# RWKV-7's 32 x 32 blocks: through DRAM and two chains, or through TensorE and one

## The chip, the cores and the metric

The kernel runs on one core of a Trainium2 chip. The metric is the device time of one execution in microseconds (us). Engines: TensorE (PE; its weight loads are PEld), VectorE (DVE), ScalarE (ACT), GpSimd (POOL) and SyncE (SP), each with its own queue of instructions in order. The program is written against a framework that fixes, before the run, in which order each engine gets its instructions: what is written first has priority, and what is written later is moved into the gaps that the framework expects.

## The reference

The input x is [1, 512, 1024]: 512 tokens of 1024 features. A first block has three branches behind one projection (a state space branch, RWKV-7 and HGRN-2), gates, an output projection and a feed-forward part; two layers of a second block with four other branches follow. The change lies in RWKV-7 alone: 8 heads of 64 features, forward and backward over the tokens.

```
def step(s, inp):
    r_t, w_t, k_t, v_t, kk_t, a_t = inp
    sa = jnp.einsum('bhvk,bhk->bhv', s, -kk_t)
    s = (s * w_t[:, :, None, :] + sa[..., None] * (kk_t * a_t)[:, :, None, :]
         + v_t[..., None] * k_t[:, :, None, :])
    return s, jnp.einsum('bhvk,bhk->bhv', s, r_t)
```

In chunks of 64 tokens this becomes products of matrices, with one inverse per chunk, head and direction: (I + A)^-1, where A is strictly triangular, 64 x 64.

## The kernel before

The stage under study runs from about 30 to 690 us of 3645. `rwkv` handles four tiles j of two heads. For each: `rwkv_in` (projections, normalised keys), `rwkv_decays`, `rwkv_mid` (all causal products of the 8 chunks and the inverses), `rwkv_scan` (8 chunks one after the other, both directions side by side) and `rwkv_out`. The inputs of tile j + 1 are written inside the scan of tile j. Behind all of RWKV, in lower priority, stand four heads of `hgrn` and 16 tiles of `gates` with tiles and PSUM banks of their own (bg, H): they fill gaps. The next stage (`ssd`) takes over the memory of this one.

In `rwkv_mid`, G[128, 32, 128] holds for each of 32 matrices m (direction, chunk, head) the products of sources i (partitions) by targets t (L424, L427). The two 32 x 32 diagonal blocks q of each 64 x 64 part have to be inverted. Forward substitution wants one block per partition, with all its elements in a row:

- L432: two DMAs write the blocks of G into the DRAM array pd; L441: two DMAs read them into M, block (q, m) on a partition, and again on the other 64 partitions.
- X0 and X1 (L436 to L443) begin as the unit matrix. Rows 4 a + 2 c + q of the inverse: c names one of two independent chains, q the half of the partitions.
- L458 to L466: for each of 31 columns i, both chains multiply (L463, into tx0, tx1) and both subtract (L466): 120 instructions of VectorE, products of column i of X with row i of M, inner runs of neighbours.
- L470: four DMAs write X to pd2; L473: two DMAs read it back into G, element (r, m, t) to partition r.
- L475 to L491: the block above the diagonal, -X1 A12 X2, for 16 matrices at a time: 16 transposes (L480) and a copy (L482) give X1 transposed, then 16 products (L485), a scaled copy (L487), 16 products (L490), a copy into G (L491).

Memory of a bank (512 float32 columns in PSUM) comes by use: S has two banks, T, O and H one, acc one.

Of the kernel before, what the change touches and what calls it, by code (L numbers as in the profile page):

```python
# [32 lines left out]
def blocks(*ws):  # L33
    """[K, N] matrices with N a multiple of 128 -> units of 8 blocks of 128 x 128, each
    unit with its rows on the partitions; the blocks run over columns, then rows."""
    seq = []
    for w in ws:
        k, n = w.shape
        seq.append(w.reshape(k // 128, 128, n // 128, 128).transpose(2, 0, 1, 3).reshape(-1, 128, 128))
    b = np.concatenate(seq) if len(seq) > 1 else seq[0]  # L40
    return np.ascontiguousarray(b.reshape(-1, UB, 128, 128).transpose(0, 2, 1, 3))


def paired(a, b):
    """Blocks of two matrices, a column tile of each in turn."""
    k, n = a.shape
    s = np.stack([w.reshape(k // 128, 128, n // 128, 128).transpose(2, 0, 1, 3) for w in (a, b)], axis=1)
    s = s.reshape(-1, UB, 128, 128)
    return np.ascontiguousarray(s.transpose(0, 2, 1, 3))


def parts(n):
    """(from, how many) of n pairs of row tiles, up to four at a time."""
# [4 lines left out]
def sevens(w0, w1):  # L58
    """Pairs of column tiles, one of each matrix [K, N]: for up to four pairs of row tiles
    (even, odd) at a time, the first tile's even and the second's even blocks, then the second's  # L60
    odd and the first's odd blocks, with the rows on the partitions."""
# [9 lines left out]
def gate_up(a, name, *ws):  # L71
    """The column tiles FF7 for products in sevens, the others for plain ones."""
# [5 lines left out]
def odd_even(w):  # L78
    """The odd and the even column tiles."""
# [5 lines left out]
#: Column tiles of the second block's w_in (without the 16 mLSTM gates) in the order of use.  # L85
# [9 lines left out]
#: The same for the first block's (without the 32 steps of the state space branch).  # L95
# [8 lines left out]
def first_constants():  # L104
    """Selectors of heads and masks of the chunks' orders."""
# [16 lines left out]
class Packed:  # L122
    """Small vectors side by side in one array; the program finds them by name."""
# [33 lines left out]
def nat_masks():  # L157
    """0 inside the window of 16 columns, -1e30 outside: 128 queries (16 columns by 8 rows) by
    256 keys (32 columns by 8 rows), for the first, the middle and the last query tiles."""
# [10 lines left out]
def arrange(x):  # L170
    """The kernel's inputs as the program reads them."""
# [55 lines left out]
def run(gen):  # L227
    """A generator's work at once; its result."""
# [6 lines left out]
class First:  # L235
    """The first block's layer: state space (SSD), RWKV-7 and HGRN-2 branches."""
# [4 lines left out]
    def conv_pad(self, ps, side):  # L241
        """psum / rms with zeros on either side."""
# [8 lines left out]
    def shifted(self, it, n, out):  # L251
        """Token shift in both directions of column tile n."""
# [6 lines left out]
    def half_sigmoid(self, out, ps, hb):  # L259
        """0.5 + 0.5 tanh: the sigmoid of (psum / WS + bias), hb half the bias."""  # L260
# [14 lines left out]
    def rwkv(self, yd):  # L275
        """Chunks of 64 tokens, both directions side by side, a tile of two heads after the
        other; the backward direction keeps its keys and values reversed within the chunks."""
# [46 lines left out]
    def rwkv_in(self, j, it, lx):  # L324
        """What a tile of two heads needs of the projections."""
# [37 lines left out]
    def rwkv_decays(self, j, lx):  # L363
        """exp of the decays' running sums (and of their negatives) as seen from the middle of
        a chunk, |exponent| < 19.5; the state's scale from one chunk's middle to the next's."""
# [30 lines left out]
    def rwkv_mid(self, j):  # L396
        """Keys and queries with their decays, all causal products of a chunk, (I + A)^-1."""
# [17 lines left out]
        # (source: b or k, i) x (target: kk or r, t) for every direction, chunk and head  # L415
# [12 lines left out]
        # the 32 x 32 diagonal blocks of I + A inverted, one block's even or odd rows a partition  # L428
        pd = self.t(self.dram, [2, 32, 32, 32], "pd")
        for q in range(2):  # L430
            s = slice(32 * q, 32 * q + 32)
            nc.scalar.dma_start(out=pd[q].rearrange("m i t -> i m t"), in_=G[s, :, s])  # L432
        M = self.t(mid, [128, 1024], "M").rearrange("p (i t) -> p i t", i=32)
        tx = [self.t(mid, [128, 80], f"tx{c}") for c in range(2)]
        # rows 4 a + 2 c + q: two independent chains c, each on the halves q of the partitions
        X = [self.t(mid, [128, 8, 32], f"X{c}") for c in range(2)]  # L436
        for c in range(2):
            nc.gpsimd.memset(X[c], 0.0)
        for q in range(2):
            s = slice(64 * q, 64 * q + 64)  # L440
            (nc.scalar, nc.sync)[q].dma_start(out=M[s], in_=pd.rearrange("q m i t -> (q m) i t"))  # L441
            for c in range(2):
                nc.gpsimd.memset(X[c].rearrange("p a b -> p (a b)")[s, 2 * c + q::36], 1.0)  # L443
        # values by token on the upper partitions
# [13 lines left out]
        for i in range(31):  # L458
            ts, nt = slice(i + 1, 32), 31 - i
            rs = [(c, (i - 2 * c) // 4 + 1) for c in range(2) if i >= 2 * c]  # L460
            for c, n in rs:
                t = tx[c][:, 0:n * nt].rearrange("p (a b) -> p a b", b=nt)
                v.tensor_tensor(out=t, in0=X[c][:, 0:n, i:i + 1].to_broadcast([128, n, nt]), in1=M[:, i:i + 1, ts].to_broadcast([128, n, nt]), op=ALU.mult)  # L463
            for c, n in rs:
                t = tx[c][:, 0:n * nt].rearrange("p (a b) -> p a b", b=nt)
                v.tensor_tensor(out=X[c][:, 0:n, ts], in0=X[c][:, 0:n, ts], in1=t, op=ALU.subtract)  # L466
        pd2 = self.t(self.dram, [2, 32, 8, 2, 2, 32], "pd2")
        for q in range(2):
            for c in range(2):
                nc.scalar.dma_start(out=pd2[:, :, :, c, q].rearrange("q m r t -> (q m) r t"), in_=X[c][64 * q:64 * q + 64])  # L470
        for q in range(2):
            s = slice(32 * q, 32 * q + 32)
            nc.scalar.dma_start(out=G[s, :, s], in_=pd2[q].rearrange("m r c e t -> (r c e) m t"))  # L473
        # the block above the diagonal: -X1 A12 X2
        lo, hi = slice(0, 32), slice(32, 64)  # L475
        for q in range(2):
            ms = range(16 * q, 16 * q + 16)
            px = self.b("S")
            for n, m in enumerate(ms):
                nc.tensor.transpose(px[lo, 32 * n:32 * n + 32], G[lo, m, lo], self.ident[lo, lo])  # L480
            st = self.w()
            nc.scalar.copy(out=st[lo], in_=px[lo])  # L482
            px = self.b("S")
            for n, m in enumerate(ms):
                mm(px[hi, 32 * n:32 * n + 32], lhsT=G[lo, m, hi], rhs=st[lo, 32 * n:32 * n + 32], start=True, stop=True)  # L485
# [8 lines left out]
    def rwkv_scan(self, j):  # L494
# [10 lines left out]
        for c in range(NC):  # L505
# [9 lines left out]
            # B v + K z = -(I + A) u on the lower, B' v + R z on the upper partitions  # L515
# [13 lines left out]
            if not last:  # L529
                # the next state, one head's values beside the other's, zero across heads  # L530
# [1617 lines left out]
```

## Time and profile before

| | |
|---|---|
| median of 3 runs | 3642.4 us (3641.06 to 3648.86) |
| profiled execution: span from first to last instruction | 3644.9 us |
| TensorE busy | 3388.2 us, 93% |
| VectorE busy | 2751.5 us, 75% |
| ScalarE busy | 1624.4 us, 45% |
| GpSimd busy | 751.7 us, 21% |

The profiled execution has no time beside its span, which already lies 2.5 us above the median. Busy time of TensorE counts from a product's start to the modelled end, overlaps once. A group "<-" names what ended the idle time before an instruction.

### The profile page before, as it was taken

What the parts mean: (1) busy time and instruction counts of PE and PEld (TensorE: products, weight loads), DVE (VectorE), ACT (ScalarE), POOL (GpSimd) and SP (SyncE); (2) the same over time, 40 slices, a digit from 0 to 9 for tenths busy, and PEclk for the clock granted to TensorE, in tenths of its full rate; (3) what the DMA queues carried; (4) which work ended last, traced back from release to release, by engine and by line L of the source; (5) the groups of instructions that cost most, each with busy time, mean ns of one, the idle gap of its engine ahead of it and who ended that gap; (6) DMA issues with size and microseconds to landing.
All of it is one profiled execution on the core that took longest, in us unless ns stands there. A gap on an engine that the chain in (4) does not pass through costs nothing. (4 is left out here: it accounts for less than half of the span.)

```text
span 3644.9 us, 60827 instructions
## 1 busy us (share of the span) xinstructions
PE 3388.2 (93%) x23758; PEld 2045.0 (56%) x23758; DVE 2751.5 (75%) x5599; ACT 1624.4 (45%) x3033; POOL 751.7 (21%) x762
## 2 busy tenths in 40 slices
PE   7899898898899999999989999999999989999998
PEld 3566565554445567655545545568655545545567
DVE  6767867587577798688767677788688767767788
ACT  4232232455444444364456544444364456634344
POOL 1322223223332212101110131211101120132211
PEclk9897999999999999999999999999999999999999
DMA  4211212333352234322323353335322323353233
GB/s 137 70 49 40 64 40 63 131 111 113 106 171 94 97 99 142 108 74 75 106 76 100 106 170 99 98 112 159 106 73 72 105 81 101 108 172 123 94 99 98
DMA packets 151157, 368.17 MB, mean 101 GB/s; under 512 B 44098, under 2 KB 47428, under 8 KB 150868
## 3 DMA queue, kind: packets, MB, share of 16 engines
q1 hardware_dynamic: 117492, 336.03, 29.5%
q0 software_dynamic: 7680, 23.00, 1.9%
q10 hardware_dynamic: 25696, 5.25, 0.8%
q8 instruction: 186, 3.05, 0.3%
q14 instruction: 103, 0.84, 0.1%
HBM read 322.72 MB, written 40.04 MB: 100 GB/s over the span
## 5 line engine op out<-in xcount | busy, mean ns | idle before, releaser
L1169 PE MATMUL acc<-xh,whi 128*128 128x512 f16 x1224 | 469.3, 383 | 33.0 <-DVE w L753 11.8
L1171 PE MATMUL acc<-xh,wlo 128*128 128x512 f16 x1224 | 469.1, 383 | 20.6 <-DVE wlo L1059 20.3
L1170 PE MATMUL acc<-xl,whi 128*128 128x512 f16 x1224 | 469.6, 384 | 0.0
L1058 ACT ACTIVATE whi<-wst 128x1024 f16<-128x1024 f32 x240 | 250.0, 1049 | 263.4 <-PE acc L1170 141.7
L1059 DVE SCALAR_TENSOR_TENSOR wlo<-wst,whi 128x1024 f16<-128x1024 f32 x240 | 319.0, 1329 | 15.4 <-ACT whi L1058 14.9
L1169 PE MATMUL bg<-xh,bhi 128*128 128x512 f16 x788 | 311.1, 395 | 9.9 <-DVE hi L811 8.2
L1171 PE MATMUL bg<-xh,blo 128*128 128x512 f16 x788 | 310.5, 394 | 5.8 <-DVE reset L309 3.2
L1170 PE MATMUL bg<-xl,bhi 128*128 128x512 f16 x788 | 311.1, 395 | 0.0
L1171 PEld LDWEIGHTS <-wlo 128*128 128x128 f16 x1632 | 160.7, 98 | 232.5 <-DVE wlo L1059 46.4
L1170 PEld LDWEIGHTS <-whi 128*128 128x128 f16 x1632 | 160.5, 98 | 213.0 <-issue 41.6
L1169 PEld LDWEIGHTS <-whi 128*128 128x128 f16 x1632 | 161.1, 99 | 193.8 <-ACT whi L1058 13.5
L1428 POOL TENSOR_TENSOR w<-w,w 128x512 f32<-128x512 f32 x66 | 117.0, 1773 | 445.4 <-DVE w L1428 280.1
L1059 DVE SCALAR_TENSOR_TENSOR blo<-bst,bhi 128x1024 f16<-128x1024 f32 (+1 forms) x156 | 180.5, 1162 | 34.4 <-ACT bhi L1058 32.7
L1204 PE MATMUL acc<-whi,xh 128*128 128x128 f16 x1152 | 195.1, 219 | 2.1 <-DVE bias L1843 1.2
L1058 ACT ACTIVATE bhi<-bst 128x1024 f16<-128x1024 f32 (+1 forms) x156 | 136.4, 887 | 133.0 <-PE bg L1170 95.7
L1206 PE MATMUL acc<-whi,xl 128*128 128x128 f16 x1152 | 195.0, 219 | 0.0
L1205 PE MATMUL acc<-wlo,xh 128*128 128x128 f16 x1152 | 195.0, 219 | 0.0
L1171 PEld LDWEIGHTS <-blo 128*128 128x128 f16 x1172 | 117.0, 100 | 131.3 <-issue 16.3
L1170 PEld LDWEIGHTS <-bhi 128*128 128x128 f16 x1172 | 117.1, 100 | 130.7 <-issue 29.0
L1169 PEld LDWEIGHTS <-bhi 128*128 128x128 f16 x1172 | 117.3, 100 | 114.7 <-issue 15.1
L1204 PEld LDWEIGHTS <-xh 128*128 128x128 f16 x1408 | 139.9, 99 | 15.2 <-issue 5.0
L1205 PEld LDWEIGHTS <-xh 128*128 128x128 f16 x1408 | 140.0, 99 | 6.8 <-issue 5.0
(665 smaller groups left out, 9117.2 us busy)
## 6 DMA issues: line engine op xcount, KB each, us to landing
wst<-win SPq DMA_DIRECT2D x92, 512.0 KB, 3.6
bst<-win SPq DMA_DIRECT2D x64, 512.0 KB, 3.7
wst<-wff SPq DMA_DIRECT2D x60, 512.0 KB, 3.6
bst<-w SPq DMA_DIRECT2D x44, 512.0 KB, 3.5
gd<-bw SPq DMA_DIRECT2D x88, 256.0 KB, 2.1
ug<-gd SPq DMA_DIRECT2D x88, 256.0 KB, 2.7
wst<-w SPq DMA_DIRECT2D x34, 512.0 KB, 3.5
wst<-wf SPq DMA_DIRECT2D x30, 512.0 KB, 3.4
```

What stands on the lines that cost most here:

```text
L1058: nc.scalar.activation(out=hi[:, h], in_=st[:, h], func=AF.Copy, scale=WS)
L1059: nc.vector.scalar_tensor_tensor(out=lo[:, h], in0=st[:, h], scalar=WS, in1=hi[:, h], op0=ALU.mult, op1=ALU.subtract)
L1169: mm(ps, lhsT=wh, rhs=h[:, k, :], start=(k == 0), stop=False)
L1170: mm(ps, lhsT=wh, rhs=l[:, k, :], start=False, stop=False)
L1171: mm(ps, lhsT=wl, rhs=h[:, k, :], start=False, stop=(k == nk - 1))
L1204: mm(o, lhsT=xh, rhs=wh, start=(k == 0), stop=False)
L1205: mm(o, lhsT=xh, rhs=wl, start=False, stop=False)
L1206: mm(o, lhsT=xl, rhs=wh, start=False, stop=(k == 7))
L1428: tt = lambda eng, o, x, y, op=ALU.add: eng.tensor_tensor(out=o, in0=x, in1=y, op=op)
```

## The change

G is turned on TensorE. A product with weights G[:, :, column] (128 partitions by 32 matrices) and 32 columns of the unit matrix puts column t of block q of all 32 matrices on 32 partitions of a bank; 64 such products fill two banks, and four copies on ScalarE bring them to M, for both halves of the partitions. M now has t outside and i inside (`(t i)`), so for one row i the neighbours in t are 32 elements apart. X is one array of 1056 columns, t outside and r inside; a partition half h keeps rows 2 a + h, in odd columns. The 31 steps have one multiplication and one subtraction each, over up to 16 rows at once.

Behind the chain 16 products with weights X[:, o:o + 128] and the unit matrix bring four columns t of all rows to 128 partitions, the rows of both halves adding up; eight copies put them into G. 32 products with weights X[:, row] give the first blocks transposed, and two copies bring them into the first 32 partitions of M, in place of L480 and L482. The space kept for GpSimd's DMA descriptors is set to 4096 bytes a partition. Comments and docstrings go too; the lines below leave these out.

```diff
-        pd = self.t(self.dram, [2, 32, 32, 32], "pd")
-        for q in range(2):
-            s = slice(32 * q, 32 * q + 32)
-            nc.scalar.dma_start(out=pd[q].rearrange("m i t -> i m t"), in_=G[s, :, s])
-        M = self.t(mid, [128, 1024], "M").rearrange("p (i t) -> p i t", i=32)
-        tx = [self.t(mid, [128, 80], f"tx{c}") for c in range(2)]
-        X = [self.t(mid, [128, 8, 32], f"X{c}") for c in range(2)]
-        for c in range(2):
-            nc.gpsimd.memset(X[c], 0.0)
-        for q in range(2):
-            s = slice(64 * q, 64 * q + 64)
-            (nc.scalar, nc.sync)[q].dma_start(out=M[s], in_=pd.rearrange("q m i t -> (q m) i t"))
-            for c in range(2):
-                nc.gpsimd.memset(X[c].rearrange("p a b -> p (a b)")[s, 2 * c + q::36], 1.0)
+        M = self.t(mid, [128, 1024], "M")
+        for u in range(2):
+            ps = self.b("S")
+            for t in range(16):
+                for q in range(2):
+                    s = slice(32 * q, 32 * q + 32)
+                    mm(ps[s, 32 * t:32 * t + 32], lhsT=G[:, :, 32 * q + 16 * u + t], rhs=self.ident[:, s], start=True, stop=True)
+            for h in range(2):
+                nc.scalar.copy(out=M[64 * h:64 * h + 64, 512 * u:512 * u + 512], in_=ps[0:64])
+        Mv = M.rearrange("p (t i) -> p i t", i=32)
+        tx = self.t(mid, [128, 136], "tx")
+        X = self.t(mid, [128, 1056], "X")
+        nc.gpsimd.memset(X, 0.0)
+        for h in range(2):
+            nc.gpsimd.memset(X[64 * h:64 * h + 64, (1, 33)[h]:1024:66], 1.0)
+        Xv = X[:, 0:1024].rearrange("p (t r) -> p r t", r=32)
...
         for i in range(31):
-            ts, nt = slice(i + 1, 32), 31 - i
-            rs = [(c, (i - 2 * c) // 4 + 1) for c in range(2) if i >= 2 * c]
-            for c, n in rs:
-                t = tx[c][:, 0:n * nt].rearrange("p (a b) -> p a b", b=nt)
-                v.tensor_tensor(out=t, in0=X[c][:, 0:n, i:i + 1].to_broadcast([128, n, nt]), in1=M[:, i:i + 1, ts].to_broadcast([128, n, nt]), op=ALU.mult)
-            for c, n in rs:
-                t = tx[c][:, 0:n * nt].rearrange("p (a b) -> p a b", b=nt)
-                v.tensor_tensor(out=X[c][:, 0:n, ts], in0=X[c][:, 0:n, ts], in1=t, op=ALU.subtract)
-        pd2 = self.t(self.dram, [2, 32, 8, 2, 2, 32], "pd2")
-        for q in range(2):
-            for c in range(2):
-                nc.scalar.dma_start(out=pd2[:, :, :, c, q].rearrange("q m r t -> (q m) r t"), in_=X[c][64 * q:64 * q + 64])
-        for q in range(2):
-            s = slice(32 * q, 32 * q + 32)
-            nc.scalar.dma_start(out=G[s, :, s], in_=pd2[q].rearrange("m r c e t -> (r c e) m t"))
+            n, nt, rs, ts = i // 2 + 1, 31 - i, slice(1, i // 2 * 2 + 2, 2), slice(i + 1, 32)
+            t = tx[:, 0:n * nt].rearrange("p (a b) -> p a b", b=nt)
+            v.tensor_tensor(out=t, in0=Xv[:, rs, i:i + 1].to_broadcast([128, n, nt]), in1=Mv[:, i:i + 1, ts].to_broadcast([128, n, nt]), op=ALU.mult)
+            v.tensor_tensor(out=Xv[:, rs, ts], in0=Xv[:, rs, ts], in1=t, op=ALU.subtract)
+        px, pt = self.b("T"), [self.b("S") for _ in range(2)]
+        for k in range(8):
+            for h in range(2):
+                o = 128 * k + 1 - h
+                mm(px[:, 64 * k:64 * k + 64], lhsT=X[:, o:o + 128], rhs=self.ident[:, 64 * h:64 * h + 64], start=(h == 0), stop=(h == 1))
+        st = M[0:32].rearrange("p (m i) -> p i m", i=32)
+        for k in range(4):
+            p = slice(32 * k, 32 * k + 32)
+            for q in range(2):
+                s = slice(32 * q, 32 * q + 32)
+                src = px[p].rearrange("p (k q m) -> p q k m", k=8, q=2)[:, q]
+                dst = G[s, :, s].rearrange("p m (k t) -> p t k m", t=4)[:, k]
+                if q:
+                    nc.scalar.copy(out=dst, in_=src)
+                else:
+                    v.tensor_copy(out=dst, in_=src)
+        for i in range(32):
+            mm(pt[i // 16][0:32, 32 * (i % 16):32 * (i % 16) + 32], lhsT=Xv[:, i // 2 * 2 + 1], rhs=self.ident[:, 64 * (i % 2):64 * (i % 2) + 32], start=True, stop=True)
+        nc.scalar.copy(out=st[:, 0:16], in_=pt[0][0:32].rearrange("p (i m) -> p i m", m=32))
+        v.tensor_copy(out=st[:, 16:32], in_=pt[1][0:32].rearrange("p (i m) -> p i m", m=32))
+        st = M[0:32].rearrange("p (m i) -> p m i", i=32)
         lo, hi = slice(0, 32), slice(32, 64)
         for q in range(2):
             ms = range(16 * q, 16 * q + 16)
             px = self.b("S")
             for n, m in enumerate(ms):
-                nc.tensor.transpose(px[lo, 32 * n:32 * n + 32], G[lo, m, lo], self.ident[lo, lo])
-            st = self.w()
-            nc.scalar.copy(out=st[lo], in_=px[lo])
-            px = self.b("S")
-            for n, m in enumerate(ms):
-                mm(px[hi, 32 * n:32 * n + 32], lhsT=G[lo, m, hi], rhs=st[lo, 32 * n:32 * n + 32], start=True, stop=True)
+                mm(px[hi, 32 * n:32 * n + 32], lhsT=G[lo, m, hi], rhs=st[:, m], start=True, stop=True)
...
-    nc = _bacc.Bacc("TRN2", target_bir_lowering=False, num_devices=1)
+    nc = _bacc.Bacc("TRN2", target_bir_lowering=False, num_devices=1, dynamic_dma_scratch_size=4096)
```

## Rows read from the trace of the kernel before

**Rows 1.** The page's first part: span, and TensorE's busy time, share, instructions.

```profile
span 3644.9 us, 60827 instructions
...
PE 3388.2 (93%) x23758; PEld 2045.0 (56%) x23758; DVE 2751.5 (75%) x5599; ACT 1624.4 (45%) x3033; POOL 751.7 (21%) x762
```

**Rows 2.** Busy time by stretch: start:end, length, engines (instructions), granted clock, DMA share, GB/s.

```profile
90.00:175.00 85.00, 71.14 (x584) 44.82 (x583) 68.28 (x193) 19.75 (x31) 26.02 (x26) 0.86 0.25 66
175.00:244.00 69.00, 66.20 (x466) 46.83 (x465) 43.30 (x114) 22.11 (x62) 19.65 (x16) 0.98 0.10 35
244.00:315.00 71.00, 62.87 (x559) 40.80 (x557) 57.71 (x180) 20.88 (x32) 16.99 (x23) 0.90 0.32 82
315.00:394.00 79.00, 77.75 (x499) 56.58 (x498) 50.75 (x127) 21.16 (x61) 17.28 (x13) 0.83 0.03 8
394.00:465.00 71.00, 60.73 (x542) 38.39 (x540) 63.40 (x183) 21.02 (x32) 25.67 (x23) 0.90 0.34 94
...
543.00:615.00 72.00, 57.10 (x570) 37.33 (x569) 59.80 (x173) 22.78 (x39) 23.72 (x14) 0.90 0.29 77
```

**Rows 3.** Line L1309, the gates' copies, up to 800 us: durations, first and last start.

```profile
L1309 ACT COPY bw<-bg x16: 567/575/591, 132.2 to 688.6; 128x512 f32<-128x512 f32 x16
```

**Rows 4.** Longest waits of TensorE, 85 to 690 us: total, times, longest.

```profile
PE H L845 <- DVE hw L840: 15.1, 10, 3.6
PE bg L1169 <- DVE hi L811: 8.2, 1, 8.2
```

**Rows 5.** VectorE in order of time in one stretch: start, length, operation, count.

```profile
243.45 0.69 DVE L427 TENSOR_TENSOR G<-S,rwm 128x512 f32<-128x512 f32 x1 [1.12 <-PE S L424]
...
256.65 0.28 DVE L463 TENSOR_TENSOR tx<-X,M 128x31 f32<-128x31 f32 x2
...
268.10 0.37 DVE L463 TENSOR_TENSOR tx<-X,M 128x76 f32<-128x76 f32 x2
268.39 0.37 DVE L466 TENSOR_TENSOR X<-X,tx 128x76 f32<-128x76 f32 x2
...
288.36 0.17 DVE L463 TENSOR_TENSOR tx<-X,M 128x16 f32<-128x16 f32 x1
...
290.42 0.17 DVE L466 TENSOR_TENSOR X<-X,tx 128x8 f32<-128x8 f32 x1
```

**Rows 6.** ScalarE in the same stretch, with the DMAs that it issues.

```profile
288.02 3.80 ACTq L470 DMA_DIRECT2D pd<-X  x4
...
302.87 0.57 ACT L482 COPY w<-S 32x512 f32<-32x512 f32 x1 [7.40 <-PE S L480]
...
314.51 0.57 ACT L491 COPY G<-S 32x512 f32<-32x512 f32 x1 [1.03 <-PE S L490]
```

**Rows 7.** DMA issues: count, size, median us from issue to landing.

```profile
M<-pd SPq DMA_DIRECT2D x4, 256.0 KB, 4.5
...
G<-pd ACTq DMA_DIRECT2D x8, 128.0 KB, 3.2
```

**Rows 8.** TensorE in order of time; a float32 product has two records.

```profile
305.24 1.19 PE L485 MATMUL S<-w,G 32*32 32x32 f32 x32
...
308.89 0.64 PE L480 MATMUL S<-ident,G 32*32 32x32 f32 x16
309.45 0.38 PE L845 MATMUL H<-hw,hw 128*128 128x128 f32 x1
...
639.76 0.66 PE L521 MATMUL O<-uv,G 64*128 64x64 f32 x4
```

**Rows 9.** Lines with steps between elements: ns shortest/median/longest (L1623 reads, L1219 and L1221 write).

```profile
L1623 DVE TENSOR_TENSOR w<-acc,rb x6: 691/1041/1049, 1780.8 to 1937.4; 128x512 f32<-128x512 f32 x6
...
L1219 ACT ACTIVATE yh<-T x3: 2440/2442/2461, 1867.5 to 1920.4; 128x512 f16<-128x512 f32 x3
L1221 DVE TENSOR_TENSOR yl<-T,yh x3: 2451/2455/2465, 1870.0 to 1922.9; 128x512 f16<-128x512 f32 x3
```

**Rows 10.** Line L454, ScalarE's copies from PSUM without steps.

```profile
L454 ACT COPY uv<-T x16: 577/581/582, 72.7 to 552.3; 64x512 f32<-64x512 f32 x16
```

**Rows 11.** Busy time in the state space stage, columns as in rows 2.

```profile
700.00:1000.00 300.00, 275.88 (x1522) 150.18 (x1521) 216.09 (x346) 157.10 (x308) 94.81 (x94) 0.97 0.35 114
```

## The prediction

> **What bounds the kernel now.** I read the page's first part, then the stretches of the RWKV stage, then the waits of TensorE, and last one stretch instruction by instruction. TensorE is busy 93% of the span [rows 1], so a change counts only by what it adds to TensorE, or by the idle time that it gives back. The RWKV stage alternates between two kinds of stretch. From G's products to the last block above the diagonal (rwkv_mid, four times) TensorE is idle 13.9, 8.1, 10.3 and 14.9 us, 47.2 in all; in the chunk loop that follows them it is busy 96 to 98% [rows 2]. The filler is HGRN's work and the gates, traced later. It does not run out: the last gate tile is copied from its bank at 688.6 us, at the very end of the stage [rows 3]. So RWKV's own latency sets how fast the stage walks, the filler uses most of what is free, and neither has much room. The idle time of the four stretches is largely VectorE's doing: the two longest waits of TensorE in the stage are for VectorE results of HGRN, 15.1 and 8.2 us [rows 4].
>
> One such stretch, tile j = 1, takes 70.9 us [rows 5, 6]. G is complete at 244.1. Two trips through DRAM bring M to the partitions, and the chain starts at 256.65: 12.5 us. The chain ends at 290.6: 33.9 us, because other work of VectorE stands between its pairs. Writing X out and reading it back into G, and the 16 transposes behind that, last until the copy at 302.87: 12.3 us. The blocks above the diagonal end at 315.1: 12.2 us. A DMA lands 3.2 to 4.5 us after its issue [rows 7]; there are four such legs in a row.
>
> **What the change removes, adds and moves, per tile of two heads.**
>
> Removed: ten DMA issues, nine from ScalarE's queue and one from SyncE's, with both waits (12.5 and most of 12.3 us of path), and L480's 32 transposes with their two copies. The transposes take 0.64 us for 16, 0.56 to the next start [rows 8]: 1.1 us of TensorE.
>
> Added on TensorE: 64 products for M and 32 for the transposed inverse, with 32 columns on each side, and 16 products with 128 weight columns by 64. The nearest row for the small ones is L485, 16 products (32 records) in 1.19 us, 0.07 each without the tail; for the 16 it is L521, two products in 0.66 us, 0.26 each without the tail [rows 8]. That gives 4.5 + 2.2 + 4.2 - 1.1 = 9.8 us. The new weights are read with steps of 512 and 128 bytes, and no row shows a weight load with a step. The nearest is VectorE's read with a step of 256 bytes, 1041 ns for 512 elements where 691 is usual [rows 9]; with 153 ns fixed (0.17 us for 16 elements [rows 5]) that is 1.73 ns an element against 1.05. Two loads of 32 such columns are 0.11 us a product: 7.1 + 3.6 + 4.2 - 1.1 = 13.8 us. I take the middle, 11.8 us, 47 for four tiles.
>
> Changed on VectorE: the old chain has 120 instructions, two independent ones side by side; the pace is 0.29 us for a pair of 76 elements [rows 5], so 0.066 us plus 1.05 ns an element. Both chains go through 2 x 2856 elements a partition: 120 x 0.066 + 6.0 = 13.9 us. In the new one each of 62 instructions waits for the one before, so each pays its full 0.153 us: 9.5 us, and 15.5 with plain elements. But M and X now lie with 128 bytes between neighbours. With the stepped read in both it is 9.5 + 9.9 = 19.4 us. The subtraction also writes with that step. The trace shows such a write with 2-byte elements only: 2442 ns on ScalarE and 2455 on VectorE for 512, 4.5 ns an element [rows 9]. With that, 9.5 + 4.9 + 12.8 = 27.2 us. I take 27.2, since that row has the same step and the same engine, and keep 15.5 as the other end.
>
> The stepped write shows a cost in [rows 9] for 2-byte elements. [...]
>
> The way out: 16 products (4.2 us), then eight copies of 32 x 256 into G with a step of 512 bytes, four on each engine, 0.4 us each if plain (a plain 64 x 512 copy takes 0.58 [rows 10]) or 1.3 at 4.5 ns an element, then one copy of 32 x 512 on each engine, 0.58 or 2.4. Behind the first ones the 32 small products are hidden. Together 4.2 + 1.6 + 0.6 = 6.4 us, or 4.2 + 5.2 + 2.4 = 11.8; I take the second for the same reason. The way in: 64 products and two last copies, 4.5 + 1.2 = 5.7 us, or 8.3 with stepped weights; I take 7.0. The block solve loses the transposes and a copy, 12.2 - 1.2 = 11.0 us.
>
> Small things at nothing: the memset of the larger X on GpSimd lies before the chain, which waits for M anyway, and would cost under 1 us without that cover; ScalarE's four more copies (2.3 us) replace its DMA issues, four of which took 3.8 us [rows 6]; the smaller scratch space for GpSimd's DMAs touches no transfer of this stage; I price it at 0, and at one landing, 3 to 4.5 us by [rows 7], for each later GpSimd transfer that would have to wait for room.
>
> **The sum.** The new stretch: 7.0 + (33.9 + 27.2 - 13.9) + 11.8 + 11.0 = 77.0 us against 70.9, so 6.1 longer. TensorE must put 62.9 + 11.8 = 74.7 us into it [rows 2], which just fits; its idle time is used, not the stretch shortened. VectorE is asked for 57.7 + 13.3 + 7.6 = 79 of 77 us, so some HGRN work slides into the chunk loop, where VectorE has 28 of 79 us free [rows 2]. Four tiles: +24 us. Behind the wait for the chain's end the products for X queue on TensorE; what stands behind them is filler, and it is late only as long as the chain is.
>
> The other end of the sum: 5.7 + (33.9 + 15.5 - 13.9) + 6.4 + 11.0 = 58.6 us, 12.3 shorter per tile, if neither steps nor waits cost anything; TensorE then limits it (first rival).
>
> **Rivals.**
>
> Faster: the steps cost nothing, and RWKV's path is 12.3 us shorter per tile. The filler that no longer fits goes into the chunk loops, which are full, and into the state space stage, where TensorE is idle 24 of 300 us [rows 11]. So the gain is bounded by TensorE: 39 added, at most 47 + 24 given back, -32; I price it at -20, 3622. For it: four DMA legs vanish. Against it: every row with a large step shows a cost. It decides if a subtraction of some 130 elements takes under about 0.35 us.
>
> No change: TensorE's 47 us go exactly into the 47.2 us of idle time and the path stays at 71: 3642. For it: the two numbers agree. Against it: half of that idle time, 23.3 us, is a wait for HGRN on VectorE [rows 4], which gets busier.
>
> Slower by more: none of the idle time comes back, because VectorE at 79 of 77 us holds up HGRN and the next tile's inputs, and TensorE pays the upper 13.8 us a tile: +55, 3697. It decides if TensorE is still idle 10 us or more in each stretch.
>
> **How the numbers follow.** Forecast 0.43, faster 0.22, no change 0.17, slower by more 0.18. The sum is made against the profiled execution's 3644.9 us, which lies 2.5 above the median of the runs; on the median 3642.4 it gives 3666. The forecast's own range is 3652 to 3682 (the terms' middles against their ends). The range for 8 in 10 leaves out the better half of the faster case and the worst of the last: 3615 to 3705. About 0.2%, 7 us, is what a measurement here can tell from no change. Faster 0.23, same 0.17, slower 0.60: the forecast and the last case make the slower one, less a little of the forecast that ends within 7 us.
>
> **What would show it.** Each stretch from G to the last block at 75 to 79 us against 71; M's 64 products in 4.5 to 7 us; a subtraction of 136 elements at 0.6 to 0.8 us, a multiplication at 0.3 to 0.4; G's copies at 1.3 us; TensorE's busy time up by 39 to 55 us in the stage and its idle time in the four stretches down to 10 to 25 us. I am wrong if 4-byte elements with a step of 128 bytes cost what neighbours cost, or if the order on the engines, made anew around the new products, puts filler where RWKV waits.

## The result, and the profile after

The changed kernel takes 3693.4 us (median of 4 runs, 3690.05 to 3695.57); the kernel before on the same chip takes 3645.6. The ratio is 1.013, 95% interval 1.0112 to 1.0148: 1.3% slower. The forecast was slower, 3666 with a range of its own of 3652 to 3682. The direction held and so did the range for 8 in 10 (3615 to 3705); the forecast's own range and the size did not: 47.8 us lost where the sum said 20 to 24. The number is nearest to the rival "slower by more" (3697).

The page's first part for the changed kernel, which answers to [rows 1]:

```profile
span 3690.9 us, 62108 instructions
...
PE 3417.8 (93%) x24526; PEld 2075.6 (56%) x24526; DVE 2783.8 (75%) x5387; ACT 1644.7 (45%) x3061; POOL 754.6 (20%) x750
```

TensorE is busy 29.6 us longer, and the span is 46.0 us longer. Where it went is seen in the stretches, with the columns of [rows 2]. The first four rows of the changed kernel go from G's completion to the last block above the diagonal in each tile, the fifth from RWKV's last chunk to the last gate tile's copy:

```profile
106.00:173.50 67.50, 54.05 (x601) 39.96 (x600) 56.09 (x116) 15.84 (x25) 16.54 (x17) 0.85 0.11 36
...
242.60:303.80 61.20, 56.95 (x540) 34.07 (x538) 45.46 (x103) 24.04 (x37) 12.13 (x18) 0.96 0.19 66
...
370.50:450.40 79.90, 66.63 (x613) 44.09 (x611) 65.33 (x130) 23.23 (x39) 26.06 (x23) 0.83 0.12 37
...
515.20:588.60 73.40, 60.69 (x603) 41.59 (x601) 66.94 (x121) 26.61 (x52) 31.76 (x22) 0.91 0.17 58
...
635.70:726.50 90.80, 73.09 (x499) 44.06 (x496) 53.37 (x87) 27.93 (x53) 41.74 (x33) 0.91 0.29 99
```

The whole stage of the changed kernel, the same columns:

```profile
30.00:726.50 696.50, 623.40 (x5235) 420.82 (x5234) 500.12 (x1029) 222.40 (x450) 182.62 (x157) 0.93 0.15 51
```

The kernel before (neither row was shown earlier), first its tail:

```profile
667.50:689.00 21.50, 15.58 (x100) 7.59 (x99) 10.80 (x32) 7.85 (x13) 11.08 (x13) 0.84 0.37 118
```

and its whole stage:

```profile
30.00:689.00 659.00, 596.73 (x4470) 390.16 (x4468) 470.80 (x1241) 203.88 (x424) 182.18 (x167) 0.90 0.21 61
```

RWKV is not later but earlier: its last chunk ends at 635.7 us, where it was 667.5. Yet the stage ends 37.5 us later, because the tail behind RWKV grew from 21.5 to 90.8 us. HGRN and the gates fill it. HGRN's last multiplication by the output gate, four times, in the changed kernel (durations, first and last start):

```profile
L916 DVE TENSOR_TENSOR hw<-hw,hg x4: 675/684/1303, 229.5 to 709.2; 128x512 f32<-128x512 f32 x4
```

and the same line of the kernel before:

```profile
L908 DVE TENSOR_TENSOR hw<-hw,hg x4: 656/675/683, 215.7 to 646.5; 128x512 f32<-128x512 f32 x4
```

HGRN ends 63 us later, and the last of the gates with the stage: the work that is moved into gaps was left behind.

**How to split such a row.** A stage's length is TensorE's idle time (length less busy), the time lost while its granted clock was at the lower of the two levels that the traces show, 0.50 instead of 1.00 (length times 1 less the mean clock; the clock's two digits make this good to some 4 us, and it is a little too much, since idle time counts in it), and the rest, the work at full clock. In the changed kernel a 128x512 product into bg took 0.38 us at 1.00 (382 to 407 us) and 0.61 to 0.63 at 0.50 (408 to 434.8 us). Before: 659.0 = 62.3 idle + 65.9 slow + 530.8 work. After: 696.5 = 73.1 + 48.8 + 574.6. So work +44, slow -17, idle +11. Behind the stage another 8.5 us are lost. These terms say where the time lies, not what caused it; the experiments show that the two differ.

### The profile page after: what moved, and what is told of

Same layout as the page of the kernel before. It is cut to its first block, busy times and chain, and to the rows that moved or that the text cites. A ratio compares the mean times of both kernels' runs of the same rounds, so it can differ in the third digit from the quotient of the medians.

```text
span 3690.9 us, 62108 instructions
## 1 busy us (share of the span) xinstructions
PE 3417.8 (93%) x24526; PEld 2075.6 (56%) x24526; DVE 2783.8 (75%) x5387; ACT 1644.7 (45%) x3061; POOL 754.6 (20%) x750
## 5 line engine op out<-in xcount | busy, mean ns | idle before, releaser
L1212 PEld LDWEIGHTS <-xh 128*128 128x128 f16 x1408 | 138.7, 99 | 12.7 <-DVE bias L1854 2.5
```

Source lines behind the costliest of these rows:

```text
L1212: mm(o, lhsT=xh, rhs=wh, start=(k == 0), stop=False)
```

## The experiments

The theories, by the letters in the expectations: T and O, the filler that the order leaves behind RWKV sets the end (T: its idle tail, O: how much of it there is); P, TensorE's added products; C and V, VectorE's chain; L, the latency of the way in and out; D, ways and products were hidden alike; K, the granted clock; N, any edit upsets a lucky order. Two letters (OP, OK) are two theories at once.

Each comparison is with the kernel before on the same chip. Filler means HGRN and the gates. The expectations count the filler "left behind" in TensorE's queue after the last block above the diagonal, 200 us' worth of products before and 243 after. Only 75 and 138 us pass between that block and the last gate tile's copy, so these counts hold products that run later. In the traces TensorE is busy with filler there (products into the banks bg and H) for 41 us before and 97 after; the figures below are of this kind.

### First: the scratch space, and a move without work

The scratch space alone, in the kernel before:

```diff
-    nc = _bacc.Bacc("TRN2", target_bir_lowering=False, num_devices=1)
+    nc = _bacc.Bacc("TRN2", target_bir_lowering=False, num_devices=1, dynamic_dma_scratch_size=4096)
```

> The kernel before with only the scratch space for GpSimd's DMA descriptors set to 4096 bytes. All theories: 3640 to 3650, no change. A rival of its own: the smaller space holds up GpSimd's 7680 packets in some stage and is itself part of the 46 us: 3655 or more.

Ratio 1.0002 (0.9992 to 1.0011): no effect. And a move in the kernel before that changes no work, the two zm instructions written ahead of the transposes of the values:

```diff
+        zm = self.t(mid, [128, NC, 2, 2], "zm", bufs=2)
+        for e in range(2):
+            v.tensor_scalar(out=zm[:, 0:NC - 1, :, e], in0=zs[:, 0:NC - 1], scalar1=self.hsel[:, e:e + 1], scalar2=None, op0=ALU.mult)
         uv = [self.t(mid, [128, NC, 128], f"uv{d}") for d in range(2)]
...
-        zm = self.t(mid, [128, NC, 2, 2], "zm", bufs=2)
```

> The kernel before with one thing that adds and removes no work: the two small VectorE instructions that make zm are written ahead of the transposes of the values instead of behind them. Theory N (the order made for the kernel before is a lucky one, and any edit scrambles it): 3665 to 3700, as far off as the kernels with real changes. Theory O (what counts is how much of HGRN's and the gates' products the order leaves behind RWKV, and this move leaves it the same): 3636 to 3652.

Ratio 1.0000 (0.9986 to 1.0013). But the edit did not reach the order: up to 1000 us its trace shows the same instructions in the same order as the kernel before on TensorE, VectorE and GpSimd, and on ScalarE but for one that moved by a place. So it says nothing on theory N, which stays open.

### Where the filler stands

```diff
-                for s in "hghhghgg":
+                for s in "hhhhgggg":
-    ("w1", 58, 63), ("w1", 22, 26), ("w1", 63, 73), ("w1", 26, 30), ("w1", 73, 78), ("w1", 30, 38),
+    ("w1", 58, 78), ("w1", 22, 38),
```

> The changed kernel with one thing moved: all four HGRN heads are written ahead of the four tiles' worth of gates (order hhhhgggg, the weights' order with it). Theory T (the tail): in the changed kernel RWKV ends 32 us earlier and HGRN 63 us later, and TensorE is idle 17.7 us behind RWKV's last chunk (5.9 before) and slower in clock (0.91); with the heads first, products of the gates are left for that tail, so it should lose 10 to 25 us: 3670 to 3683. Theory P (TensorE's added products, 47.8 us busy, are the whole cost): within 5 us of the changed kernel, 3688 to 3698. Theory C (the pace of the single chain): no change either.

> The same move of the HGRN heads in the kernel before, as a control. Theory T: here HGRN ends 40 us before the stage does and the tail's idle time is only 5.9 us, so within 5 us of 3645. If it gains as much as the changed kernel does, the move is good by itself and says nothing of the change.

Changed kernel 1.0155 (1.0128 to 1.0183), no gain; kernel before 1.0165 (1.0144 to 1.0187), 59 us lost by the order of the filler alone, more than the whole change costs. Theory T missed in both; P's range held for the changed kernel. The granted clock of the control's stage is 0.84:

```profile
30.00:746.00 716.00, 634.80 (x4491) 423.93 (x4490) 467.98 (x1241) 204.22 (x424) 173.63 (x167) 0.84 0.20 58
```

It has 520 us of work at full clock, less than before, but 115 us of slow time and 81 idle. Next, in the changed kernel, the filler written between the tiles, same sequence (h, one head of HGRN, behind tile 0, gh behind tile 1, hg behind tile 2, hgg behind tile 3; g are gates), so that part of it has priority over the later tiles:

```diff
             self.rwkv_out(j, gx, yd)
+            self.filler(j)
...
-                for s in "hghhghgg":
```

> The changed kernel with HGRN's heads and the gates (still in the order hghhghgg) written between the tiles of RWKV, h behind tile 0, gh behind tile 1, hg behind tile 2, hgg behind tile 3, so that more of their products have priority over the later tiles. In the order of TensorE's queue the products left for behind the last block above the diagonal fall from 243 to 223 us' worth (200 in the kernel before). Theory O: the tail behind RWKV shrinks from 91 to about 70 us and the time by 10 to 25 us: 3668 to 3683. Theory K (the granted clock decides): any time from 3675 to 3715, with the loss at the low clock explaining what the tail does not. Theory N: the same spread.

> As the last, but earlier still: hg behind tile 0, hh behind tile 1, ghg behind tile 2, g behind tile 3, which leaves only 174 us' worth. Theory O: the tail is nearly gone and the stage is bound by TensorE's work: 3650 to 3680. A rival: filler that has priority over the chunk loop holds up RWKV's own chain, and the last tiles have nothing left to fill their stretches with: 3695 or more, with TensorE idle 10 us or more a stretch in the last two.

> The changed kernel with the filler between the tiles in another plan, h, gh, hgh, gg, which leaves 189 us' worth behind RWKV (223 in the first plan, 243 unchanged, 174 in the plan that lost 33 us). Theory OP: the tail falls below 35 us, but the third chunk loop is held up by 30 us more of filler: 3665 to 3690, no better than the first plan. If what counts is the tail alone: 3640 to 3660.

The first plan: 3669.2, ratio 1.0084 (1.0057 to 1.0111), about 17 us less lost than the change's 1.013, the intervals just apart, in theory O's range. Its tail:

```profile
664.00:714.50 50.50, 42.76 (x320) 23.59 (x319) 22.54 (x54) 19.99 (x41) 25.19 (x24) 0.93 0.42 145
```

and its stage:

```profile
30.00:714.50 684.50, 622.59 (x5297) 419.53 (x5296) 497.23 (x1033) 225.05 (x452) 183.35 (x158) 0.94 0.16 54
```

The tail is 40 us shorter (74 us of filler behind the last block, 97 without the move), and the chunk loop of tile 3 ends 28 us later. The plan between the two gave 1.0084 (1.0066 to 1.0101), the same, though its tail is gone: RWKV's last chunk ends at 705.6 us and the last gate copy at 706.1, and only 23 us of filler stand behind the last block, less than in the kernel before. The earliest plan (2 us) gave 1.0228 (1.0206 to 1.0249): filler held RWKV up, from tile 2's last block above the diagonal to tile 3's G 164 us passed (65 in the changed kernel), and RWKV ended at 751, as the rival of its expectation said. So some 17 us, about a third of the loss, come back when filler stands elsewhere, and no plan tried took more; the tail does not carry the rest, since without it the time is the same. The same plan was not run in the kernel before, so it is not shown that these 17 us belong to the change.

### TensorE's added products

The 112 products of a tile, put into the kernel before with G as weights and read by nothing:

```diff
+        for u in range(2):
+            ps = self.b("S")
...
+                    mm(ps[s, 32 * t:32 * t + 32], lhsT=G[:, :, 32 * q + 16 * u + t], rhs=self.ident[:, s], start=True, stop=True)
...
         pd = self.t(self.dram, [2, 32, 32, 32], "pd")
```

> The kernel before, with the change's 112 products a tile added and read by nothing (64 of 32 by 32 columns and 32 of 32 by 32 and 16 of 128 by 64, all with G as weights), the DRAM trips and the two chains left as they were. Theory P: TensorE has 96% of its time taken, so the kernel pays the products less what the clock gives back: +25 to +48 us, 3670 to 3693. Theory T: 47 us of idle time stand in the four stretches and the order of HGRN is not disturbed, so +0 to +15, 3645 to 3660. Theory C: as T.

And left out of the changed kernel, without and with the filler between the tiles:

```diff
-            for t in range(16):
+            for t in range(1):
...
-        for k in range(8):
+        for k in range(1):
...
-        for i in range(32):
+        for i in (0, 16):
```

> The changed kernel with 104 of the 112 new products of each tile left out: one 32-column product for each half bank of M and one for each half of the transposed inverse, two for X, and the copies read the same few columns again. The values behind them are not the reference's; copies, chain, waits and order stay. Theory P (TensorE's time): some 44 us of products are gone, so 3693 less 30 to 60: 3633 to 3663. [...] Theory D (DRAM's trips were hidden anyway and the products are too): within 10 us of 3693.

> The changed kernel with both edits: the filler written between the tiles, and 104 of the 112 new products of each tile left out (values behind them are not the reference's). Theory OP (the loss is filler left behind RWKV, and once that is mended TensorE's work decides): some 40 us of work less than the 3669 of the filler alone, 3625 to 3645. Theory O alone (the products fit in TensorE's idle time and cost nothing): 3660 to 3675. Theory K (the granted clock takes it back, as it did in part when the products alone were left out): 3650 to 3665 with a loss at the low clock of 55 us or more.

Added: 1.026 (1.0238 to 1.0282), 96 us, twice what any theory said. Left out (the copies stay and read the few columns that are left): 1.0142 (1.0116 to 1.0168) against 1.013, nothing, as theory D said; with the filler between 1.0067 (1.0041 to 1.0094) against 1.0084, nothing that can be told, as theory O alone said. The stage with the products added to the kernel before:

```profile
30.00:774.30 744.30, 662.04 (x5359) 448.22 (x5358) 472.92 (x1241) 202.30 (x422) 178.37 (x166) 0.87 0.18 54
```

The stage of the changed kernel with the products left out:

```profile
30.00:730.70 700.70, 610.36 (x4481) 396.27 (x4480) 495.77 (x1035) 222.64 (x452) 175.91 (x157) 0.89 0.16 53
```

The stage with the products left out and the filler between the tiles:

```profile
30.00:714.30 684.30, 601.14 (x4475) 393.79 (x4474) 491.14 (x1035) 223.27 (x452) 179.82 (x158) 0.89 0.17 54
```

This is the reading that matters most. In the second, work falls from 574.6 to 533.3, the level of the kernel before. But idle time rises by 17 and slow time by 28, and the stage is 4 us longer. In the third, against the filler alone, work falls by 56, slow rises by 34, idle by 21. Here the work that was taken away came back as waiting and as time at half clock. So the +44 of work in the account above is not by itself the cause. One way to read it is that the products stand in front of waits and cost nothing; another is that their removal gained time and the order, which is made anew in each of these kernels, lost as much. No run tells the two apart. In the first, besides the work (+34), slow (+31) and idle (+20) rose, and HGRN ended at 759 us, with 97 us of filler behind the last block: the filler ran later.

### The two halves

The changed kernel with the old way in (pd, two DMAs out, two in), and the kernel before with the new way in, the second also with the filler between:

```diff
-            for t in range(16):
-                for q in range(2):
...
+        pd = self.t(self.dram, [2, 32, 32, 32], "pd")
```

> The changed kernel with the old way in: M through DRAM in four transfers, its rows now neighbours, the new chain and the new way out kept. Theory P: TensorE loses M's 15.5 us of products: 3672 to 3682. Theory L (the latency of the way decides): the way in grows from 6 to 12.5 us, four times: 3710 to 3725. [...]

> The kernel before with the new way in alone (M's products and copies, written so that rows are neighbours); the two chains, the four transfers out of X and the two back into G, and the 16 transposes a half stay. Theory P: M's products add 15.5 us: 3650 to 3665. Theory L: 6 us a tile are saved on the way in: 3615 to 3630. Theory K: 3630 to 3680.

> The kernel before with the new way in alone (which took 3675) and the filler written between the tiles; the products left behind RWKV fall from 254 to 215 us' worth. Theory OP: M's products are 15.5 us of TensorE, the rest of its 38 us over before is the order: 3645 to 3660. Theory K: up to 3680.

1.0163 (1.0137 to 1.0189); 1.0097 (1.008 to 1.0114); and 1.0038 (1.0023 to 1.0053) with the filler. Theories P and L missed in the first two; K's wide range held in the second, and OP's in the third. The new way in shortens the four stretches to 250 us together (290 before), RWKV ends 47 us earlier, and the kernel still loses 35 us: its tail is 99 us. Latency (theory L) buys nothing here. The two kernels that keep one half of the change each lose 59 and 35 us, together twice what the whole change loses, so the halves do not add up.

### VectorE's chain

Two chains in the changed layout, every other row each; then neighbours in place of steps (t innermost in M and X, X turned by 64 products of 32 weight columns):

```diff
-            n, nt, rs, ts = i // 2 + 1, 31 - i, slice(1, i // 2 * 2 + 2, 2), slice(i + 1, 32)
+            rs = [(c, (i // 2 - c) // 2 + 1, slice(1 + 2 * c, i // 2 * 2 + 2, 4)) for c in range(2) if i // 2 >= c]
```

```diff
-        Xv = X[:, 0:1024].rearrange("p (t r) -> p r t", r=32)
+        Xv = X.rearrange("p (r t) -> p r t", t=32)
```

> The changed kernel with its rows split into two independent chains (every other row each), 122 instructions a tile instead of 62, in the changed layout. Theory C: with two chains side by side each wait is covered by the other chain and not by one HGRN instruction of 0.7 us, so the chains shorten from 50 to about 37 us a tile and the kernel gains 15 to 30 us: 3663 to 3678. Theory P: VectorE's chain is not what bounds, within 6 us of 3693. Theory T: RWKV gets further ahead of HGRN, the tail longer, 0 to +10.

> The changed kernel with t innermost in both M and X (the copies into M write with a step, X is turned by 64 products of 32 weight columns instead of 16 of 128), so that the single chain reads and writes neighbours. The chain's own instructions should fall from 20.9 to about 15.5 us a tile. Theory C (the chain's pace decides): 4 times 5 us less, 3670 to 3680. Theory O: the products left behind RWKV stay at 242 us' worth, so no gain but for a shorter RWKV: 3685 to 3698. By the steps of the prediction (the stepped write is what makes the chain long): 3665 to 3680.

> The changed kernel with two chains in its own layout (3688 alone) and the filler between the tiles (3669 alone). Theory V: both act, on different parts (the stretch, the tail): 3648 to 3662. Theory OK: 3662 to 3680. A version that beats the kernel before, under 3635, is not expected: the full-clock work of TensorE is 40 us more than there.

Two chains: 1.0125 (1.0102 to 1.0149). The stretches fell from 282 to 236 us together, as theory C said, and the tail rose to 102: no gain that can be told, as theory P said; the longer tail was theory T's. With the filler between, 1.0143 (1.0126 to 1.016); the move that gave 17 us with one chain gave nothing with two, for which no reason was found. Neighbours: 1.0179 (1.015 to 1.0207), slower, with 44 us more TensorE work than the change. Every range missed in these two; the subtraction of 136 elements is shorter, as its row (sum and mean) shows:

```profile
L465 DVE TENSOR_TENSOR X<-X,tx 128x136 f32<-128x136 f32 x4 | 1.2, 294 | 0.1
```

The changed kernel, multiplication and subtraction of 136 elements:

```profile
L463 DVE TENSOR_TENSOR tx<-X,M 128x136 f32<-128x136 f32 x4 | 1.5, 384 | 0.1
L464 DVE TENSOR_TENSOR X<-X,tx 128x136 f32<-128x136 f32 x4 | 1.5, 384 | 0.1
```

Last, every second step of the chain left out, with the filler between the tiles, and then the products too:

```diff
-        for i in range(31):
+        for i in range(0, 31, 2):
```

> The changed kernel with the filler between the tiles (3669) and every second of the 31 steps of the chain left out (the inverses are not the reference's). Theory V (VectorE's stretch from the chain's first to its last instruction sets RWKV's pace): some 10 us of the chain and half of the other work put between its steps go, 15 to 20 us a tile; TensorE's full-clock work of 588 us then limits: 3635 to 3655. Theory OK (what is left is the order and the granted clock): 3660 to 3680, with more products left behind RWKV (234 us' worth against 223).

> As the last, and 104 of the 112 products of each tile left out too. Theory V: neither engine is loaded any more, 45 us of TensorE's work are gone and 15 to 20 us a tile of VectorE's stretch: 3600 to 3635. Theory OK: 3645 to 3670, with the loss at the low clock or the idle time of TensorE over 55 us each.

1.0148 (1.0131 to 1.0166): the stretches fell to 173 us together, and the kernel became some 23 us slower than with the whole chain: RWKV ended only 8 us earlier, at 656 us, and the tail grew from 50.5 to 80 us. With the products left out too, 1.002 (1.0001 to 1.0038), the level of the kernel before. Theory V missed in both, in the first by 42 us; OK's range missed the first and held the second. The stage with half the chain:

```profile
30.00:735.90 705.90, 633.59 (x5232) 425.92 (x5231) 479.07 (x909) 223.01 (x450) 183.34 (x157) 0.92 0.15 49
```

and with half the chain and the products left out:

```profile
30.00:684.00 654.00, 586.38 (x4406) 379.06 (x4405) 464.57 (x909) 222.34 (x450) 184.64 (x157) 0.92 0.17 53
```

Here the same products, which had cost nothing beside the whole chain, are worth 47 us (1.0148 against 1.002): work falls by 43 us, and this time idle and slow time do not rise. Two limits suggest themselves, VectorE's beside the whole chain and TensorE's beside half of it, but they are not shown: by them half the chain could not be slower than the whole one, and it is, by 23 of the 47 us. Against the whole chain with its products, both removals together gain 23 us (1.0084 to 1.002). No version beats the kernel before.

## Why the prediction was right and wrong

**TensorE's price came out right, in part by luck.** The prediction took 47 us for four tiles. The new groups (count, busy, mean ns, idle before) and the transposes that went (5.1 us):

```profile
L470 PE MATMUL T<-ident,X 128*128 128x64 f32 x128 | 22.1, 301 | 13.9 <-DVE X L464 13.6
...
L435 PE MATMUL S<-ident,G 128*32 128x32 f32 x512 | 15.5, 222 | 0.0
...
L483 PE MATMUL S<-ident,X 128*32 128x32 f32 x256 | 15.3, 227 | 0.0
```

22.1 + 15.5 + 15.3 - 5.1 = 47.8. M's 64 products are 3.9 us a tile, under the 4.5 to 7 named; the 32 small ones are 3.8, above their 2.2 to 3.6, and the 16 for X 5.5, above the 4.2: the errors cancel. Busy time in the stage rose by only 26.7 (39 to 55 forecast), because the clock was higher than before (0.93 against 0.90, 17 us less of slow time by the split above), which the sum had no term for.

**The step that failed** is "its idle time is used, not the stretch shortened", with "RWKV's own latency sets how fast the stage walks". The sum let TensorE's idle time in the four stretches fall by 23 us. By the rows above it fell from 47.2 to 43.7 (13.5, 4.3, 13.3 and 12.7), and the tail added 12. The two longest waits of TensorE in the changed kernel, 85 to 735 us (total, times, longest), show what took its place:

```profile
PE H L853 <- DVE hw L848: 20.5, 10, 3.8
PE T L470 <- DVE X L464: 13.6, 14, 4.2
```

The first is the wait for HGRN on VectorE that [rows 4] shows. Before, it and the other wait of [rows 4] took 23.3 us, all in the four stretches; now it takes 11.9 us in them and 8.6 behind RWKV, and the other is gone. The second is new and lies all in the stretches: the products for X wait for the end of the chain, and TensorE with them. The prediction had said of this wait that only filler behind it is late, and had put no idle time on it. The other half of the step failed in the opposite way: the stretches did not grow by 24 us but shrank by 8, to 282, the chunk loops from 232 to 208, and the stage still ended later. RWKV's latency did not set the end; the filler, which the order put behind it, did. The prediction had seen that the last gate tile ends at the very end [rows 3], and took it as a sign that filler does not run out, not that filler was the next to be late. The rival "slower by more" came nearest with its number, but its mechanism (VectorE holds up HGRN) carries only those 11.9 us, and its mark, 10 us or more idle in each stretch, holds in three of four, as it did before the change.

**The price of the steps was too high.** The chain was given 27.2 us alone, with the subtraction's stepped write at 4.5 ns an element. The rows with 136 elements show 384 ns for multiplication and subtraction alike; less the 153 fixed that is 1.7 ns an element, against (294 - 153) / 136 = 1.04 with neighbours. So the stepped read cost what [rows 9] said, 1.7 against 1.04, and a stepped write of 4-byte elements beside it nothing more: the multiplication, which writes neighbours, took the same 384 ns. The prediction had priced the write by the row of 2-byte elements, 4.5 ns an element, and that was the wrong neighbour. The chain's instructions took 24.2 us a tile, 19.2 without what they lost beside GpSimd (last section), so the end named for a stepped read only, 19.4 us, had the price right. The copies into G took 0.60 us, nearer the plain 0.4 than the 1.3, and those into M 1.03, not 2.4.

**And yet the chain was as long as forecast, by luck.** It ran 47.2, 41.0, 59.5 and 53.5 us against the 47.2 of the sum, for another reason. The sum left 20 us of VectorE's other work in it, and the trace has 30 on average. That is one of the two signs of being wrong that it had named, filler put "where RWKV waits". VectorE in order of time in tile 0 (start, length, line):

```profile
128.37 0.39 DVE L464 TENSOR_TENSOR X<-X,tx 128x135 f32<-128x135 f32 x1
128.67 0.74 DVE L257 SCALAR_TENSOR_TENSOR fv<-xp,cols,fv 128x512 f32<-128x512 f32 x1
129.33 0.37 DVE L463 TENSOR_TENSOR tx<-X,M 128x126 f32<-128x126 f32 x1
129.62 0.67 DVE L345 COPY i<-acc 2x512 f32<-2x512 f32 x1
130.22 0.90 DVE L464 TENSOR_TENSOR X<-X,tx 128x126 f32<-128x126 f32 x1
130.97 0.68 DVE L821 TENSOR_TENSOR hg<-bg,rt 128x512 f32<-128x512 f32 x1
131.57 0.38 DVE L463 TENSOR_TENSOR tx<-X,M 128x130 f32<-128x130 f32 x1
131.86 0.69 DVE L847 TENSOR_TENSOR hw<-hq,hp 128x512 f32<-128x512 f32 x1
```

Between two dependent steps of the one chain stands one longer instruction of other work; from the chain's first to its last instruction VectorE is busy 191 of 201 us over the four tiles (127 of 138 before). In the kernel before, the two chains took turns, and of the other work 11 to 15 us a tile stood among them, not 22 to 40. The way in came to 5.8 to 6.7 us (forecast 7.0) and everything behind the chain to 13.4 to 14.4 (forecast 22.8). So a way 71 us shorter over four tiles was eaten by chains 63 us longer.

**The wait that was named** is there: the products for X stand in TensorE's queue among filler and held it for 13.6 us in all, at no price in the sum; and the eight copies into G, on two engines, take turns: in tile 0 they run one after the other from 160.3 to 166.9 us.

**What stays open.** No single cause is shown to carry the 46 us. Shown is what the runs took: some 17 us less with the filler elsewhere; nothing from the products beside the whole chain, 47 us beside half of it; 35 and 59 us lost with one half of the change each. The obvious rival is the order itself (theory N). The same instructions in another order moved the kernel before by +59 us and the changed one by -17 to +36, as far as the whole change does. And where the work was changed, the traces show the instructions that both kernels share in another order too, on TensorE and on VectorE. No run holds the order fixed while the work changes, so how much of the loss is the work and how much the order is not known. Not settled either is why the filler between gave nothing with two chains, why half the chain alone cost 23 us, how the slow time (28 to 115 us in these stages) follows from the order, and what the 8.5 us behind the stage are (2964 us from the last gate copy to the end, 2956 before, 2952 with the filler between).

## What to carry to other kernels

When a path is shortened in a kernel whose gaps are full, ask first where the filler will go that lived in those gaps, and what ends last when it stands at the end: here RWKV came 32 us earlier and the stage 37 us later. Before a dependent chain of short instructions replaces two that cover each other, look at what else its engine holds, because a scheduler fills each wait with something longer. Test a cost by taking it away as well as by adding it: the 112 products a tile cost 96 us when added, gave nothing when removed, and gave 47 when removed beside half of the chain. And where the order on the engines is made anew for each edit, compare it in the traces: a neutral edit is a control for the order only if it changes it.

## What the runs showed of the hardware

Small VectorE instructions lasted until a GpSimd instruction beside them had ended: of the chain's, 19 took over 0.6 us in the changed kernel (0.75 to 2.18), and each of them ended 0.03 to 0.24 us after a GpSimd instruction that had run beside it. One is a subtraction of 16 elements (0.17 us for a multiplication of as many [rows 5]):

```profile
156.38 2.65 POOL L1063 TENSOR_TENSOR blo<-bst,bhi 128x1024 f16<-128x1024 f32 x1
156.97 2.09 DVE L464 TENSOR_TENSOR X<-X,tx 128x16 f32<-128x16 f32 x1
```

The 70 instructions of the chain (of 248) that overlap GpSimd's take 41.7 of its 96.9 us, some 20 more than their like do alone; in the kernel before, 19 us went the same way. In the rows above both end at 159.0 to 159.1 us.

TensorE's granted clock is a large term of its own: from 0.84 (the kernel before with the heads first) to 0.96 (neighbours in the chain) over the stage in the kernels run here. One fall in the changed kernel, within a chain: the 20 us before it, the stretch itself, and the 20 us behind it.

```profile
388.00:408.00 20.00, 17.99 (x94) 9.31 (x93) 20.00 (x42) 4.94 (x7) 5.26 (x3) 0.99 0.17 54
408.00:435.00 27.00, 17.64 (x85) 11.02 (x85) 22.55 (x46) 3.97 (x9) 11.65 (x9) 0.50 0.13 39
435.00:455.00 20.00, 19.59 (x276) 16.60 (x274) 9.50 (x23) 7.87 (x22) 2.17 (x4) 1.00 0.01 2
```

VectorE, with the chain and other work, is busy all of the 20 us before and 84% of the 27. TensorE, 90% busy before the fall, then runs at the lower level, 0.50, and 65% busy; the clock is back at 1.00 from 435 us, and the chain is over at 436.
